# A hybrid retention, S5 and cross-attention block: who issues the rope's swap transfers, when the retention transposes are written, and the S5 matrices made in two halves

## The chip, the cores and the metric

The kernel runs on one core of one Trainium2 chip. The core has TensorE (PE, matrix products), VectorE (DVE), ScalarE (ACT), GpSimd (POOL) and SyncE (SP), which here does nothing but issue transfers. Each engine works through its own instructions in a fixed order. The metric is the device time of one execution in microseconds (us).

## The reference

One layer on x of 1024 x 1024 in float32, cut to what matters here:

```
h = rms_norm(x, norm1_g);  q, k, v, g_ret, u, g_s5 = split(h @ w_in)
q, k = rotary(q), rotary(k)              # 8 heads of 64: x1*cos - x2*sin, x1*sin + x2*cos
ret = group_norm(retention(q, k, v)) * silu(g_ret)     # chunks of 128, v heads of 128
ssm = s5(u) * silu(g_s5)                 # 64 groups of 16 channels, 64 complex states each
x = x + concat([ret, ssm]) @ w_out
x = x + cross_attention(rms_norm(x), rms_norm(mem)) @ xa_wo
return rms_norm(x, norm_f_g)
```

In S5, each group has its own discretised transition (`abar`), input matrix (`f * b`) and output matrix `c`. The kernel turns these into small matrices over blocks of time steps: powers of `abar` times B and times C, and the short convolution kernels that follow from both.

## The kernel before

All large products are made of three TensorE passes over a high and a low part of the operands (`mm3`, lines 95 to 97; `whi_`/`wlo_` are the two parts of a weight, made by ScalarE on line 74 and by VectorE or GpSimd on line 75).

A loop `for i in range(4)` goes over pairs of heads; the text calls its passes pair 0 to pair 3. Each pass projects k (`kps`) and q (`qps`), applies the rope to both, projects v (`vps`, 2 x 96 matmuls) and the gate (`gps`, 2 x 96), and then calls `retention`. The rope evicts the projection to `qs` (ACT, line 290), makes `sw`, a copy whose 32-row blocks are swapped in pairs, by four transfers (line 294), and combines them on DVE (lines 296 to 298). `retention` transposes k (`knps`), forms the chunk states (`kvps`, then `R` on DVE), the scores (`scps`, masked to `st` on DVE), the outputs (`ops`, evicted to `o` by ACT on line 536), the group norm (`mv`, `rs`, `nb`), scales `o` in 16 ACT instructions (line 554), multiplies by the gate on DVE (line 555), transposes the result (`rtps`, line 559) and stores it (`ret_d`).

`s5_prep(b)` makes the S5 matrices of block b (16 blocks of 4 groups). `s5_tables(ct)`, called at every second block, makes on POOL a table of powers (`tab`, lines 307 to 414), stores it (`tab_d`, line 417), clears a small tile (`z`, line 419) and stores that. The next table overwrites `tab`, so it starts when `tab_d` has landed. For each b POOL makes `B`, `C` and `t`; DVE makes `W` (lines 455, 457) and `VV`; PE transposes `W` (`mps`, line 460) and multiplies B by VV (`kps` with `VV`, line 470); ACT and DVE finish `Mi` and `K`. Blocks 0 to 3 are written behind pair 0's retention, 4 to 8 behind pair 1's, 9 to 13 behind pair 2's, 14 and 15 behind pair 3's. After the loop the u projection (`ups`) and the S5 scan start.

The code's order is not the order on the engines: a scheduler reorders each engine's instructions at build time, so that retention i lies under the projections of pair i+1, its `rtps` in the middle of that pair's `vps`, and S5 blocks after them. On the chip every engine keeps that order and waits in place. SP issues nearly all transfers, in one order. Transfers take one of eight completion semaphores in turn, and a transfer waits for the earlier one that holds its semaphore.

Of the kernel before, what the change touches and what calls it, by code (L numbers as in the profile page):

```python
# [12 lines left out]
F32 = mybir.dt.float32  # L13
# [7 lines left out]
P = 128  # L21
# [24 lines left out]
def block_kernel(ctx: ExitStack, tc: tile.TileContext, a: dict):  # L46
# [3 lines left out]
    def bc(ap, shape):  # L50
        return ap.to_broadcast(shape)
# [10 lines left out]
    def sm_ps(shape, name="smps"):  # L62
        return psm.tile(shape, F32, tag="sm", name=name)
# [223 lines left out]
    def rope(ps, name):  # L287
        flat = ps.rearrange("p a b -> p (a b)")
        qs = qp.tile([P, L], F32, tag="qs", name=f"qs_{name}", bufs=2)
        s.activation(qs, flat, AF.Copy)  # L290
        sw = qp.tile([P, L], F32, tag="qsw", name=f"sw_{name}", bufs=2)
        for b in range(4):
            o = 32 * (b ^ 1)
            nc.sync.dma_start(out=sw[32 * b:32 * b + 32, :], in_=qs[o:o + 32, :])
        rot = qp.tile([P, L], F32, tag="rot", name=f"rot_{name}", bufs=3)
        v.tensor_tensor(rot, qs, cosT, ALU.mult)
        v.tensor_tensor(sw, sw, sinT, ALU.mult)
        last_rope[0] = v.tensor_tensor(rot, rot, sw, ALU.add)
        return rot
# [109 lines left out]
    def s5_tables(ct):  # L409
        raw = pr.tile([P, 2, 4, GB, 16], F32, tag="bcraw", name=f"bcraw{ct}", bufs=2)  # L410
        nc.sync.dma_start(out=raw, in_=a["s5_bc"][ct])
        tab = pr.tile([P, 2, GB, SC], F32, tag="tab", name=f"tab{ct}")
        g.tensor_copy(tab[:, 0, :, 0:16], rotC[:, ct])
        g.tensor_copy(tab[:, 1, :, 0:16], rotS[:, ct])
        scr = pr.tile([P, 256], F32, tag="tg", name=f"tg{ct}")
        rotate_double(tab[:, 0], tab[:, 1], 16, SC, scr, 4)
        nc.sync.dma_start(out=a["tab_d"][ct], in_=tab)
        zero = pr.tile([P, 2, 112], F32, tag="tg", name=f"z{ct}")
        g.memset(zero, 0.0)
        nc.sync.dma_start(out=a["k_d"][ct].rearrange("(h p) t -> p h t", h=2)[:, :, 0:112], in_=zero)  # L420
        per_ct[ct] = raw

    def s5_prep(b):
        gs = slice(b * GB, b * GB + GB)
        ct, hb = b // 2, b % 2
        if hb == 0:
            s5_tables(ct)
        raw = per_ct[ct][:, hb]
        B1 = pr.tile([P, GB + 1, 16], F32, tag="B1", name=f"B1_{b}", bufs=2)
        B2 = pr.tile([P, GB, 16], F32, tag="B2", name=f"B2_{b}")  # L430
        C1 = pr.tile([P, GB, 16], F32, tag="C1", name=f"C1_{b}")
        tt = pr.tile([P, GB, 16], F32, tag="tt16", name=f"tt16_{b}")
        sh = [P, GB, 16]

        def fb(x):
            return bc(x[:, gs].unsqueeze(2), sh)
        g.memset(B1[:, GB, :], 0.0)
        g.tensor_tensor(B1[:, 0:GB], raw[:, 0], fb(FR), ALU.mult)
        g.tensor_tensor(tt, raw[:, 1], fb(FIs), ALU.mult)
        g.tensor_tensor(B1[:, 0:GB], B1[:, 0:GB], tt, ALU.add)  # L440
        g.tensor_tensor(B2, raw[:, 1], fb(FRs), ALU.mult)
        g.tensor_tensor(tt, raw[:, 0], fb(FI), ALU.mult)
        g.tensor_tensor(B2, B2, tt, ALU.subtract)
        g.tensor_scalar(C1, raw[:, 2], psgn, None, op0=ALU.mult)

        def pw(tab, n):
            return bc(tab[:, 0:n, gs].rearrange("p t g -> p g t").unsqueeze(3), [P, GB, n, 16])

        def ve(x, n):
            return bc(x.unsqueeze(2), [P, GB, n, 16])  # L450
        W1 = pr.tile([P, GB, 8, 16], F32, tag="W1", name=f"W1_{b}")
        t1 = pr.tile([P, GB, 8, 16], F32, tag="t1", name=f"t1_{b}")
        VV = pr.tile([P, GB, 9, 16], F32, tag="VV", name=f"VV_{b}", bufs=2)
        t2 = pr.tile([P, GB, 9, 16], F32, tag="t2", name=f"t2_{b}")
        v.tensor_tensor(W1, pw(PR, 8), ve(B1[:, 0:GB], 8), ALU.mult)
        g.tensor_tensor(t1, pw(PI, 8), ve(B2, 8), ALU.mult)
        v.tensor_tensor(W1, W1, t1, ALU.add)
        mp = sm_ps([P, GB, P], "mps")
        for gi in range(GB):
            nc.tensor.transpose(mp[:, gi, :], W1[:, gi].rearrange("p t q -> p (t q)"), ident)  # L460
        Mi = pr.tile([P, GB, P], F32, tag="Mi", name=f"Mi_{b}", bufs=2)
        s.activation(Mi, mp, AF.Copy)
        nc.sync.dma_start(out=a["mi_d"][b], in_=Mi)
        v.tensor_tensor(VV, pw(PR, 9), ve(C1, 9), ALU.mult)
        v.tensor_tensor(t2, pw(PI, 9), ve(raw[:, 3], 9), ALU.mult)
        v.tensor_tensor(VV, VV, t2, ALU.subtract)
        nc.sync.dma_start(out=a["vv_d"][b], in_=VV.rearrange("p g t q -> p g (t q)"))
        kp = sm_ps([P, P], "kps")
        for gi in range(GB):
            nc.tensor.matmul(kp[32 * gi:32 * gi + 32, :], B1[:, gi:gi + 2, :].rearrange("p g q -> p (g q)"),  # L470
                             VV[:, gi, 0:8, :].rearrange("p t q -> p (t q)"), start=True, stop=True)
        K = pr.tile([P, P], F32, tag="K", name=f"K_{b}", bufs=2)
        s.activation(K, kp, AF.Copy)
        v.scalar_tensor_tensor(K[:, 0:16], i16, d4[:, b:b + 1], K[:, 0:16], op0=ALU.mult, op1=ALU.add)
        nc.sync.dma_start(out=a["k_d"][ct][P * hb:P * hb + P, 112:112 + P], in_=K)


    def proj_nat(w, name, evac):
        hi, lo = w
        for n0 in range(0, NCH, 4):  # L480
# [83 lines left out]

    for i in range(4):
        w = w0 if i == 0 else get_w("w_kq", i)
        kT = rope(proj_t(w, 0, hT, name="kps"), f"k{i}")
        qT = rope(proj_t(w, 1, hT, name="qps"), f"q{i}")
        vt = qp.tile([P, NCH, 256], F32, tag="vt", name=f"vt{i}")
        silu = qp.tile([P, NCH, 256], F32, tag="silu", name=f"silu{i}")  # L570

        def ev_v(n0, ps, vt=vt, i=i):
            for n in range(4):
                for h in range(2):
                    s.activation(vt[:, n0 + n, h * P:h * P + P], ps[:, n, h * P:h * P + P], AF.Copy,
                                 scale=vs[:, n0 + n, 2 * i + h:2 * i + h + 1])

        def ev_g(n0, ps, silu=silu):
            for n in range(4):
                s.activation(silu[:, n0 + n, :], ps[:, n, :], AF.Silu, scale=r1[:, n0 + n:n0 + n + 1])  # L580

        proj_nat(get_w("w_v", i), "vps", ev_v)
        proj_nat(get_w("w_g", i), "gps", ev_g)
        retention(i, kT, qT, vt, silu)
        if i == 0:
            with tc.issue_after(last_rope[0].ins):
                s5_params()
        for b in range((0, 4, 9, 14)[i], (4, 9, 14, 16)[i]):
            s5_prep(b)
    qctx.close()  # L590
    prctx.close()

# [509 lines left out]

# [14 lines left out]
```

## Time and profile before

| | |
|---|---|
| three runs | 1187.71, 1185.93, 1185.98 us; median 1185.98 |
| profiled execution | 1183.76 us, span of its trace 1182.0 us |
| busy: PE, DVE, ACT, POOL | 1132.4 (96%), 640.4 (54%), 451.0 (38%), 284.6 (24%) us |
| mean granted TensorE clock | 0.979 of full speed |

The span is the time from the first to the last instruction of the trace; all positions below are us from its start. Busy time of PE counts matmuls at whatever clock they ran, so a stall is visible as idle time and a slow stretch as a granted clock below 1.

### The profile page before, as it was taken

Reading aid. Unit: us, or ns where it says so; the run is one execution under the profiler, and the core shown is the slowest. Engines: PE = TensorE matmul, PEld = TensorE weight load, DVE = VectorE, ACT = ScalarE, POOL = GpSimd, SP = SyncE. Lnnn points to the kernel's source line nnn. Section 1 sums busy time; section 2 is a strip of 40 time slices with the busy share of each in tenths; the row PEclk is TensorE's granted clock in tenths of the full one; section 3 lists DMA queues with packets and bytes.
Section 4 is the critical chain, followed back from the end, with each engine's and each line's share of the span. In section 5 each row is a group of like instructions: output and inputs, shape, how many; then the busy total and the mean of one; then the engine's idle time right before and its main releaser. Section 6 shows DMA issues by size and latency. Waiting matters only on the chain.

```text
span 1182.0 us, 18361 instructions
## 1 busy us (share of the span) xinstructions
PE 1132.4 (96%) x7020; PEld 991.8 (84%) x7020; DVE 640.4 (54%) x1348; ACT 451.0 (38%) x903; POOL 284.6 (24%) x422
## 2 busy tenths in 40 slices
PE   8899689999999689999999999999999999999996
PEld 6897688898888568888888888888889888889996
DVE  7794464573662425585577216534635445554564
ACT  7322432342432312354453115224334444444453
POOL 2348798372084101212221100000320000000000
PEclk9899899999999889999999999999999999999998
DMA  6412343343241177799785349534446522222251
GB/s 233 120 52 89 98 159 131 101 153 97 55 165 58 36 225 202 212 279 276 222 268 202 133 148 279 179 124 148 137 143 197 173 77 72 72 72 72 90 197 72
DMA packets 92376, 171.88 MB, mean 145 GB/s; under 512 B 10880, under 2 KB 46976, under 8 KB 92288
## 3 DMA queue, kind: packets, MB, share of 16 engines
q1 hardware_dynamic: 92000, 170.57, 45.7%
q8 instruction: 55, 0.90, 0.3%
q14 instruction: 33, 0.27, 0.1%
q10 hardware_dynamic: 288, 0.14, 0.0%
HBM read 122.04 MB, written 44.43 MB: 141 GB/s over the span
## 4 chain that ended last, share of the span: by engine, by line
PE 59%; DMA 2%; DVE 2%; ACT 1%; issue 0%; DVEq 0%; ACTq 0%
PE wops L95 3%; PE wops L96 3%; PE wops L97 3%; PE qaps L97 3%; PE qaps L96 3%; PE gsps L97 2%; PE glups L95 2%; PE glups L97 2%; PE qaps L95 2%; PE gsps L96 2%; PE gsps L95 2%; PE obps L96 2%; PE obps L95 2%; PE obps L97 2%; PE glups L96 2%; PE oaps L97 2%
## 5 line engine op out<-in xcount | busy, mean ns | idle before, releaser
L95 PE MATMUL vps<-whi_w_v,hh 128*128 128x256 f32 x256 | 73.5, 287 | 0.7 <-ACT qs_k L290 0.7
L96 PE MATMUL vps<-wlo_w_v,hh 128*128 128x256 f32 x256 | 73.5, 287 | 0.6 <-POOL wlo_w_v L75 0.6
L95 PE MATMUL wops<-whi_w_xo,o 128*128 128x256 f32 x256 | 73.6, 288 | 0.0
L97 PE MATMUL vps<-whi_w_v,hl 128*128 128x256 f32 x256 | 73.5, 287 | 0.0
L97 PE MATMUL wops<-whi_w_xo,o 128*128 128x256 f32 x256 | 72.1, 281 | 0.0
L95 PE MATMUL gps<-whi_w_g,hh 128*128 128x256 f32 x256 | 71.9, 281 | 0.0
L96 PE MATMUL wops<-wlo_w_xo,o 128*128 128x256 f32 x256 | 71.8, 281 | 0.0
L97 PE MATMUL gps<-whi_w_g,hl 128*128 128x256 f32 x256 | 71.8, 281 | 0.0
L96 PE MATMUL gps<-wlo_w_g,hh 128*128 128x256 f32 x256 | 71.5, 279 | 0.0
L844 POOL TENSOR_TENSOR sq<-sq,sqx 128x1024 f32<-128x1024 f32 x7 | 19.0, 2717 | 196.9 <-ACT sqx L843 196.9
L95 PE MATMUL ups<-hh,whi_w_u 128*128 128x512 f32 x128 | 51.9, 406 | 1.9 <-DVE ut L692 1.9
L95 PEld LDWEIGHTS vps<-whi_w_v,hh 128*128 128x128 f32 x256 | 49.8, 194 | 1.8 <-ACT qs_k L290 1.1
L96 PE MATMUL ups<-hl,whi_w_u 128*128 128x512 f32 x128 | 51.2, 400 | 0.0
L97 PE MATMUL ups<-hh,wlo_w_u 128*128 128x512 f32 x128 | 51.2, 400 | 0.0
L96 PEld LDWEIGHTS vps<-wlo_w_v,hh 128*128 128x128 f32 x256 | 49.8, 195 | 1.6 <-POOL wlo_w_v L75 0.8
L95 PE MATMUL oaps<-reth,whi_w_oa 128*128 128x512 f32 x128 | 51.0, 398 | 0.0
L97 PE MATMUL qaps<-h,wlo_w_xq 128*128 128x512 f32 x128 | 50.6, 396 | 0.0
L95 PE MATMUL gsps<-hh,whi_w_gs 128*128 128x512 f32 x128 | 50.6, 395 | 0.0
L97 PE MATMUL gsps<-hh,wlo_w_gs 128*128 128x512 f32 x128 | 50.6, 395 | 0.0
L95 PE MATMUL qaps<-h,whi_w_xq 128*128 128x512 f32 x128 | 50.5, 394 | 0.0
L96 PE MATMUL qaps<-h,whi_w_xq 128*128 128x512 f32 x128 | 50.4, 394 | 0.0
L97 PE MATMUL oaps<-reth,wlo_w_oa 128*128 128x512 f32 x128 | 50.3, 393 | 0.0
(394 smaller groups left out, 3496.2 us busy)
## 6 DMA issues: line engine op xcount, KB each, us to landing
CS<-tab_d SPq DMA_DIRECT2D x32, 256.0 KB, 5.2
yr<-y_d SPq DMA_DIRECT2D x16, 512.0 KB, 6.2
wraw_w_xq<-w_xq SPq DMA_DIRECT2D x16, 512.0 KB, 4.1
wraw_w_xo<-w_xo SPq DMA_DIRECT2D x16, 512.0 KB, 4.4
vv_d<-VV SPq DMA_DIRECT2D x16, 288.0 KB, 2.8
VV<-vv_d SPq DMA_DIRECT2D x16, 288.0 KB, 4.3
wraw_w_v<-w_v SPq DMA_DIRECT2D x8, 512.0 KB, 4.6
wraw_w_g<-w_g SPq DMA_DIRECT2D x8, 512.0 KB, 4.8
```

What stands on the lines that cost most here:

```text
L95: nc.tensor.matmul(out, wh, xh, start=first, stop=False)
L96: nc.tensor.matmul(out, wh, xl, start=False, stop=False)
L97: nc.tensor.matmul(out, wl, xh, start=False, stop=last)
L844: g.tensor_tensor(sq2, sq2, sq, ALU.add)
```

## The change

Three edits. In `rope` the four swap transfers are issued by ScalarE, not SyncE. `retention` ends with the gated `o`; its transposes and stores are a new function `ret_store`, called in the next pass behind that pair's k projection (for pair 3 behind the first u projection, which is written before it). `s5_prep` is cut in two: the new `s5_prep` makes W and VV, `s5_finish` does the PE part and the stores, and `s5_hook`, called at sixteen points of the projections of pairs 1 to 3 and once behind the loop, finishes block b-1 and prepares block b. POOL's `B` and `C` are made once for two blocks, inside `s5_tables`. A reserved scratch area shrinks from 1024 to 512 bytes.

```diff
-            nc.sync.dma_start(out=sw[32 * b:32 * b + 32, :], in_=qs[o:o + 32, :])
+            nc.scalar.dma_start(out=sw[32 * b:32 * b + 32, :], in_=qs[o:o + 32, :])
...
-        per_ct[ct] = raw
+        gs = slice(ct * 2 * GB, ct * 2 * GB + 2 * GB)
+        sh = [P, 2, GB, 16]
+        B1 = pr.tile([P, 2 * GB + 1, 16], F32, tag="B1", name=f"B1_{ct}", bufs=2)
...
+        g.tensor_tensor(b1, raw[:, :, 0], fb(FR), ALU.mult)
...
+        per_ct[ct] = raw, B1, B2, C1
...
+        v.tensor_tensor(VV, VV, t2, ALU.subtract)
+        return W1, VV, B1
+
+    def s5_finish(b, prep):
+        W1, VV, B1 = prep
...
+    def s5_hook():
+        b = sdone[0]
+        sdone[0] += 1
+        if 0 < b <= NB:
+            s5_finish(b - 1, spreps.pop(b - 1))
+        if b < NB:
+            spreps[b] = s5_prep(b)
...
             evac(n0, ps)
+            hook()
...
             v.tensor_tensor(o[:, h], o[:, h], silu[:, :, h * P:h * P + P], ALU.mult)
+        return o
+
+    def ret_store(i, o):
+        for h in range(2):
...
         kT = rope(proj_t(w, 0, hT, name="kps"), f"k{i}")
+        if i:
+            ret_store(i - 1, o_last)
+        hook = s5_hook if i >= 1 else no_hook
+        if i >= 2:
+            hook()
         qT = rope(proj_t(w, 1, hT, name="qps"), f"q{i}")
+        if i >= 2:
+            hook()
...
-        for b in range((0, 4, 9, 14)[i], (4, 9, 14, 16)[i]):
-            s5_prep(b)
+    w_u0 = get_w("w_u", 0)
+    u_first = proj_t(w_u0, 0, hT, name="ups")
+    ret_store(3, o_last)
+    s5_hook()
```

What stands on the engines shows three places. First SP before, in pair 1, from the table that is stored ahead of the q rope's swap (`sw_q_1628`) to the one behind it; `kq_50` is a load of the next pair's k and q weights:

```order
L417 DMA tab_d<-tab_2303 128x1024
L420 DMA k_d<-z_2326 128x2x112
L70 DMA wraw_w_kq_50_1865<-w_kq 128x1024
L294 DMA sw_q_1628<-qs_q_1626 32x1024 x4
L70 DMA wraw_w_kq_51_1871<-w_kq 128x1024
```

and ACT after, at the same place:

```order
L290 ACTIVATE qs_q_1410<-qps 128x1024
L294 DMA sw_q_1412<-qs_q_1410 32x1024 x4
L577 ACTIVATE o_923<-o_923,nb_1041,rs_1040 128x128 x16
L613 ACTIVATE vt_1421<-vps,vs 128x128 x8
```

The four transfers have left SP's order, where a table's store stood ahead of them, and stand on ACT directly behind the eviction that they read, ahead of the 16 scalings.

Second, PE in the changed kernel from pair 1's retention transposes on (of `rtps` and `mps` alone; 17 `vps` stand between the two `rtps` rows, and the rest of the `vps` or 96 `gps` before each `mps`):

```order
L586 MATMUL rtps<-cp,o_923 128x128 x8
L586 MATMUL rtps<-cp,o_923 128x128 x8
L475 MATMUL mps<-cp,W_0_1582 128x128 x4
L475 MATMUL mps<-cp,W_1_1715 128x128 x4
L475 MATMUL mps<-cp,W_2_1898 128x128 x4
```

The first `rtps` stands behind 122 `vps` before and behind 125 after, so `ret_store` moves nothing much on PE. Of the S5 blocks, pair 1's projections now hold three (four before), pair 2's six (five), pair 3's six (five), the end of the loop one (two), and they stand farther apart.

Third, DVE after, from block 3's `W` to the second masked score `st` of pair 1's retention, which lies under pair 2's k and q projections:

```order
L462 TENSOR_TENSOR W_3_2027<-PR,B_1_1886 128x512
L465 TENSOR_TENSOR VV_2393<-PR,C_2_2381 128x576
L464 TENSOR_TENSOR W_3_2027<-W_3_2027,t_3_2028 128x512
L467 TENSOR_TENSOR VV_2393<-VV_2393,t_4_2394 128x576
L75 TENSOR_TENSOR wlo_w_v_6_2228<-wraw_w_v_60_2229,whi_w_v_6_2227 128x512 x2
L466 TENSOR_TENSOR t_5_2482<-PI,bcraw_2351 128x576
L75 TENSOR_TENSOR wlo_w_v_6_2228<-wraw_w_v_61_2235,whi_w_v_6_2227 128x512 x2
L486 SCALAR_TENSOR_TENSOR K_2023<-cp,K_2023 128x16
L529 SCALAR_TENSOR_TENSOR R_2050<-R_2050,cp 128x128 x4
L544 TENSOR_TENSOR st_2087<-scps,cp 128x512
L529 SCALAR_TENSOR_TENSOR R_2050<-R_2050,cp 128x128
L544 TENSOR_TENSOR st_2089<-scps,cp 128x512
```

Before, blocks 3 and 4 both stood ahead of `R` there. POOL now makes `t_3` behind the sixth table, two places behind its `z`:

```order
L441 TENSOR_SCALAR C_2_2381<-bcraw_2351,cp 128x128
L419 MEMSET z_3462 128x224
L463 TENSOR_TENSOR t_3_2028<-PI,B_1_1887 128x512
```

So a wait for `t_3` now stands ahead of `R` and `st`; and POOL's order is the first five tables, `t_2`, the sixth table, `t_3`, then the seventh (with `t_4` near its end) and the eighth.

## Rows read from the trace of the kernel before

**Rows 1.** Waits of PE: engine, what waits, for whom: us, times, longest

```profile
PE rtps L559 <- DVE o L555: 22.0, 3, 10.6
PE mps L460 <- DVE W L457: 5.8, 3, 3.3
PE ups L95 <- DVE ut L692: 1.9, 1, 1.9
...
PE mps L460 <- DVE K L474: 1.4, 1, 1.4
PE ops L531 <- DVE mv L540: 1.3, 1, 1.3
```

**Rows 2.** Timeline of PE: start, us, instruction, idle before it and its releaser

```profile
148.78 1.97 PE L559 MATMUL rtps<-cp,o 128*128 128x128 f32 x8 [10.57 <-DVE o L555]
...
238.43 1.03 PE L559 MATMUL rtps<-cp,o 128*128 128x128 f32 x8
```

**Rows 3.** Timeline of DVE in pair 1

```profile
112.58 1.44 DVE L297 TENSOR_TENSOR sw_k<-sw_k,sinT 128x1024 f32<-128x1024 f32 x1 [7.79 <-DMA sw_k<-qs_k]
...
132.66 0.66 DVE L550 SCALAR_TENSOR_TENSOR nb<-mv,rs 128x16 f32<-128x16 f32 x1
144.13 1.37 DVE L297 TENSOR_TENSOR sw_q<-sw_q,sinT 128x1024 f32<-128x1024 f32 x1 [10.81 <-DMA sw_q<-qs_q]
...
147.09 3.30 DVE L555 TENSOR_TENSOR o<-o,silu 128x1024 f32<-128x1024 f32 x2
```

**Rows 4.** Timeline of SP in pair 1 (issue of transfers)

```profile
134.83 0.32 SPq L417 DMA_DIRECT2D tab_d<-tab  x1
...
136.61 2.74 SPq L294 DMA_DIRECT2D sw_q<-qs_q  x4
```

**Rows 5.** Timeline of ACT: its first transfer, and pairs 1 and 2

```profile
0.74 0.41 ACTq L188 DMA_DIRECT2D gp<-g  x1
...
126.28 1.01 ACT L290 ACTIVATE qs_q<-qps 128x1024 f32<-128x1024 f32 x1
133.41 6.31 ACT L554 ACTIVATE o<-o,nb,rs 128x128 f32<-128x128 f32 x16 [6.13 <-DVE nb L550]
...
209.12 1.09 ACT L536 ACTIVATE o<-ops 128x512 f32<-128x512 f32 x2 [4.23 <-PE ops L534]
```

**Rows 6.** Windows: us, busy PE (x) PEld (x) DVE (x) ACT (x) POOL (x), PEclk, DMA share, GB/s

```profile
149.00:152.00 3.00, 3.00 (x17) 3.00 (x17) 1.39 (x1) 1.38 (x2) 0.60 (x2) 0.56 0.60 217
...
356.00:360.00 4.00, 4.00 (x21) 4.00 (x22) 2.83 (x5) 0.49 (x2) 3.91 (x6) 0.57 0.19 70
```

**Rows 7.** Timeline of POOL: starts and ends of tables; a `t`

```profile
123.08 0.24 POOL L413 COPY tab<-rotC 128x64 f32<-128x64 f32 x1 [2.47 <-DMA tab_d<-tab]
...
134.87 0.29 POOL L419 MEMSET z<- 128x224 f32 x1
...
152.08 0.24 POOL L413 COPY tab<-rotC 128x64 f32<-128x64 f32 x1 [2.42 <-DMA tab_d<-tab]
...
171.06 0.28 POOL L419 MEMSET z<- 128x224 f32 x1
...
352.96 1.10 POOL L456 TENSOR_TENSOR t<-PI,B 128x512 f32<-128x512 f32 x1
```

**Rows 8.** Timeline of PE, pair 1's retention under pair 2's projections

```profile
188.78 1.03 PE L494 MATMUL knps<-cp,rot_k 128*128 128x128 f32 x8
...
205.49 1.05 PE L531 MATMUL ops<-vt,st 128*128 128x128 f32 x8
...
216.67 0.38 PE L531 MATMUL ops<-vt,st 128*128 128x128 f32 x2
```

**Rows 9.** Timeline of DVE, pair 1's retention and later

```profile
199.41 2.05 DVE L506 SCALAR_TENSOR_TENSOR R<-R,cp 128x128 f32<-128x128 f32 x4 [4.65 <-ACT R L504]
...
214.65 0.65 DVE L521 TENSOR_TENSOR st<-scps,cp 128x512 f32<-128x512 f32 x1
...
250.09 0.78 DVE L457 TENSOR_TENSOR W<-W,t 128x512 f32<-128x512 f32 x1
```

More of the change, by code (lines that the diff above doesn't have):

```diff
@@ L420, in s5_tables, with fb, hg @@
         nc.sync.dma_start(out=a["k_d"][ct].rearrange("(h p) t -> p h t", h=2)[:, :, 0:112], in_=zero)
-        per_ct[ct] = raw
+        gs = slice(ct * 2 * GB, ct * 2 * GB + 2 * GB)
+        sh = [P, 2, GB, 16]
+        B1 = pr.tile([P, 2 * GB + 1, 16], F32, tag="B1", name=f"B1_{ct}", bufs=2)
+        B2 = pr.tile([P, 2 * GB, 16], F32, tag="B2", name=f"B2_{ct}")
+        C1 = pr.tile([P, 2 * GB, 16], F32, tag="C1", name=f"C1_{ct}")
+        tt = pr.tile([P, 2, GB, 16], F32, tag="tt16", name=f"tt16_{ct}")
+        def fb(x):
+            return bc(x[:, gs].rearrange("p (h g) -> p h g", h=2).unsqueeze(3), sh)
+        def hg(x):
+            return x.rearrange("p (h g) q -> p h g q", h=2)
+        b1, b2 = hg(B1[:, 0:2 * GB]), hg(B2)
+        g.memset(B1[:, 2 * GB, :], 0.0)
+        g.tensor_tensor(b1, raw[:, :, 0], fb(FR), ALU.mult)
+        g.tensor_tensor(tt, raw[:, :, 1], fb(FIs), ALU.mult)
+        g.tensor_tensor(b1, b1, tt, ALU.add)
+        g.tensor_tensor(b2, raw[:, :, 1], fb(FRs), ALU.mult)
+        g.tensor_tensor(tt, raw[:, :, 0], fb(FI), ALU.mult)
+        g.tensor_tensor(b2, b2, tt, ALU.subtract)
+        g.tensor_scalar(hg(C1), raw[:, :, 2], psgn, None, op0=ALU.mult)
+        per_ct[ct] = raw, B1, B2, C1
     def s5_prep(b):
@@ L427, in s5_prep @@
             s5_tables(ct)
[L428 to L444, printed above, removed]
+        raw, B1, B2, C1 = per_ct[ct]
+        ks = slice(hb * GB, hb * GB + GB)
+        raw, B2, C1 = raw[:, hb], B2[:, ks], C1[:, ks]
         def pw(tab, n):
@@ L454, in s5_prep @@
         t2 = pr.tile([P, GB, 9, 16], F32, tag="t2", name=f"t2_{b}")
-        v.tensor_tensor(W1, pw(PR, 8), ve(B1[:, 0:GB], 8), ALU.mult)
+        v.tensor_tensor(W1, pw(PR, 8), ve(B1[:, ks], 8), ALU.mult)
         g.tensor_tensor(t1, pw(PI, 8), ve(B2, 8), ALU.mult)
         v.tensor_tensor(W1, W1, t1, ALU.add)
+        v.tensor_tensor(VV, pw(PR, 9), ve(C1, 9), ALU.mult)
+        v.tensor_tensor(t2, pw(PI, 9), ve(raw[:, 3], 9), ALU.mult)
+        v.tensor_tensor(VV, VV, t2, ALU.subtract)
+        return W1, VV, B1
+    def s5_finish(b, prep):
+        W1, VV, B1 = prep
+        ct, hb = b // 2, b % 2
         mp = sm_ps([P, GB, P], "mps")
@@ L463, in s5_prep @@
         nc.sync.dma_start(out=a["mi_d"][b], in_=Mi)
-        v.tensor_tensor(VV, pw(PR, 9), ve(C1, 9), ALU.mult)
-        v.tensor_tensor(t2, pw(PI, 9), ve(raw[:, 3], 9), ALU.mult)
-        v.tensor_tensor(VV, VV, t2, ALU.subtract)
         nc.sync.dma_start(out=a["vv_d"][b], in_=VV.rearrange("p g t q -> p g (t q)"))
@@ L469, in s5_prep @@
         for gi in range(GB):
-            nc.tensor.matmul(kp[32 * gi:32 * gi + 32, :], B1[:, gi:gi + 2, :].rearrange("p g q -> p (g q)"),
+            nc.tensor.matmul(kp[32 * gi:32 * gi + 32, :], B1[:, hb * GB + gi:hb * GB + gi + 2, :].rearrange("p g q -> p (g q)"),
                              VV[:, gi, 0:8, :].rearrange("p t q -> p (t q)"), start=True, stop=True)
@@ L475, in s5_prep, with proj_nat @@
         nc.sync.dma_start(out=a["k_d"][ct][P * hb:P * hb + P, 112:112 + P], in_=K)
-    def proj_nat(w, name, evac):
+    spreps, sdone = {}, [0]
+    def s5_hook():
[5 more added lines that the diff above has]
+            spreps[b] = s5_prep(b)
+    def proj_nat(w, name, evac, hook):
         hi, lo = w
@@ L563, in retention, with no_hook @@
                                   in_=rt.rearrange("p a b -> p (a b)"))
+    def no_hook():
+        pass
+    o_last = None
     for i in range(4):
@@ L580, in ev_g @@
                 s.activation(silu[:, n0 + n, :], ps[:, n, :], AF.Silu, scale=r1[:, n0 + n:n0 + n + 1])
-        proj_nat(get_w("w_v", i), "vps", ev_v)
-        proj_nat(get_w("w_g", i), "gps", ev_g)
-        retention(i, kT, qT, vt, silu)
+        proj_nat(get_w("w_v", i), "vps", ev_v, hook)
+        proj_nat(get_w("w_g", i), "gps", ev_g, hook)
+        o_last = retention(i, kT, qT, vt, silu)
         if i == 0:
@@ L684, in block_kernel @@
     for gi in range(4):
-        w = get_w("w_u", gi)
+        w = get_w("w_u", gi) if gi else w_u0
         for c in range(2):
             ct = 2 * gi + c
-            ps = proj_t(w, c, hT, name="ups")
+            ps = proj_t(w, c, hT, name="ups") if ct else u_first
             ut = ev.tile([P, 8, 8, 16], F32, tag="ut", name=f"ut{ct}", bufs=3)
@@ L1104 @@
     arrays = host_arrays(**inputs)
-    nc = bacc.Bacc("TRN2", target_bir_lowering=False, num_devices=1, dynamic_dma_scratch_size=1024)
+    nc = bacc.Bacc("TRN2", target_bir_lowering=False, num_devices=1, dynamic_dma_scratch_size=512)
     aps = {n: nc.dram_tensor(n, z.shape, mybir.dt.from_np(z.dtype), kind="ExternalInput").ap()
```

## The prediction

> **What bounds the kernel.** PE is busy for nearly the whole span, so a change can gain only where PE waits, or where it runs slowly after a wait. I read the waits of PE first. Three waits of the retention transposes for DVE's gated `o` make 22.0 us, three waits of S5 transposes for `W` 5.8, and single waits of `ups`, `mps` (for `K`) and `ops` 1.9, 1.4 and 1.3 [rows 1]. The timeline of PE puts the longest but one detail at pair 1: 10.57 us before the transposes at 148.78 [rows 2]. Going back from there, DVE multiplied `o` by the gate from 147.09, and had stood 10.81 us in front of `sw_q` until 144.13 [rows 3]. ACT had made the transfers' input by 127.29 (126.28 + 1.01) [rows 5]. SP issued them only at 136.61, behind a table's store that waited for POOL until 134.83 [rows 4]. So the chain is POOL's table, SP's order, the swap, DVE, PE. ACT's 16 scalings were finished at 139.72 [rows 5] and were not what was late.
>
> PE pays once more behind a stall: from 149 to 152 its granted clock is 0.56, that is mostly at the lower of its two levels, 1.2 instead of 2.4 GHz, having been idle before it. This costs 3.0 x 0.44 = 1.3 us. From 356 to 360, behind the 3.3 us wait of an `mps`, it is 0.57: 1.7 us [rows 6].
>
> **The swaps on ScalarE, pair 1.** Four transfers behind `qs_q` at 0.41 us each (ACT's own issue) are out by 129 [rows 5]. SP needed 2.74 for four [rows 4]; were ACT as slow it would be 130. They landed 4.8 us after SP's last issue in pair 1 (139.35 to 144.13) [rows 3, 4], so `sw_q` is there by 134 to 135 at the latest, near DVE's `nb`, which ends at 133.32 [rows 3]. ACT's scalings start on `nb`, not on the transfers [rows 5]. `sw_k`, for which DVE waited 7.79 us [rows 3], comes earlier too, and the 1.3 us wait of `ops` [rows 1] and all behind it with it, `nb` and the scalings too: the first head is scaled half-way through 6.31 us, at 135.3, the second at 138.4. A gating takes 1.65 (3.30 for two) [rows 3], and DVE's remaining rope addition of about as long lies between the two: gated at 137.0 and 140.2. PE reaches the first `rtps` at 138.21 (148.78 - 10.57) - 1.3 + 0.3 (three more `vps`) = 137.2 and the second, 8 transposes of 1.03 [rows 2] and 17 `vps` later, at about 140.2. So the stall goes: -10.6, -1.3 of slow clock, -1.3 of `ops` = **-13.2**. Bounds: -8 if the transfers land 5 us later than I take, and nothing beyond -13.2.
>
> Here a rule speaks against the change. The row shows that moving the issue takes the swap out of a queue where it stood 9.3 us (127.29 to 136.61) [rows 4, 5]. The Trainium skill (DMA: Bandwidth & Descriptors, "Issuing engines are not separate DMA queues") says that transfers started by several engines run on the same DMA engines, and that issuing from more of them saves only the issuer's own time, usually small beside the transfer. By that rule pair 1 would gain the 2.74 us of issue and not 10.6; what stood in the queue here was a wait for POOL and no transfer, so I go by the rows and keep the other as a rival.
>
> In pairs 0, 2 and 3 PE waits for no rope transfer [rows 1], so the swaps there gain 0. SP's freed time gains nothing either.
>
> **The retention transposes.** PE's order shows them after 125 `vps` instead of 122: nothing, since the scheduler had already put them there. In the tail the stall of 10.2 us has the same order before and after and stays.
>
> **The S5 halves.** Of the three waits of `mps` for `W`, two (together 5.8 - 3.3 = 2.5 us) are in pair 1, where blocks followed each other every few us; 96 matmuls now lie between them: **-2.5** (0 to -2.5). The third is in pair 3, at a `W` that waited for POOL's `t` at 352.96 [rows 7], behind seven small `B`/`C` instructions and two `wlo_w_u`. The wider instructions leave about 3.5 us less ahead of `t_13`: of the 3.3 and the 1.7 of slow clock I take **-4.0** (0 to -5). In the tail one block is left, so the 1.4 of `mps` for `K` and part of the 1.9 of `ups`, whose DVE input stood behind that `K`, can go: **-1.4** (0 to -3.3). The PE work itself is moved, not removed.
>
> **What it gives back.** PE reaches pair 1's `knps` at 188.78 [rows 8] less 13.2, 2.5 and one block of about 1 us that has moved on: 172.1. `ops` then wants its masked scores at 205.49 - 16.7 = 188.8, and the second `ops` at 216.67 - 16.7 = 200.0 [rows 8]. But POOL does not come earlier: nothing of its table chain hung on PE. A table takes 11.8 us (123.08 to 134.87) plus 2.7 for its store to land [rows 7]. The fifth starts at 152.08 [rows 7] and so ends near 163.9; `t_2` follows; the sixth starts at 166.6, with some 1.5 us of `B`/`C` ends at 179.9, and `t_3` at about 181.2. DVE, which had stood for `t_3`, then has W, VV, `t_5` and four `wlo` at 0.78 each, 5.5 us, `R` 2.8 and two `st` of 0.65 [rows 9]: the second `st` is ready at 190.8, 2.0 us too late (two tables stand ahead of it: 0 if they take 10.8, 4 if they take 12.8).
>
> A second wait is not in the diff. The program's semaphores make the fourth `sw_k` transfer of pair 2, now on ACT, wait until the seventh table's store has landed, and the evictions of `ops` stand behind it. The seventh table starts at 182.6, holds two more POOL instructions of 1.5 us together, ends near 195.9 and has landed near 198.6. The evictions, wanted at 194, then start at 199. From the eviction to the second `st` of the next half took 6.2 us (209.12 to 215.30) [rows 5, 9]: 205.2, against 200.0 + 2.0: 3.2 us more (0 to 6). The eighth table's store, on which `sw_q` of pair 2 depends in the same way, should have landed at 213, before its `qs_q` is ready (`ops` at 202 and more than 10 us of projection): 0. With 1 us of slow clock behind the two waits (0 to 3) the give-back is **+6.2** (0 to 13).
>
> **The sum.** -13.2 - 2.5 - 4.0 - 1.4 + 6.2 = -14.9. The profiled execution took 1183.76 us, 2.2 less than the median of the runs, 1185.98; I subtract from the median: 1171.1, and 1168.9 for a profiled run.
>
> **Rivals.**
> - *No give-back.* If the tables run some 1.7 us faster each (three stand ahead of the 5.2 us), both waits in pair 2 vanish: 1171.1 - 6.2 = 1164.9, and with the S5 waits gone in full 1162. For it: POOL no longer has as many small instructions among its tables. Against it: the next table waits for the store of the last, and POOL shares time with a DVE that is now busier earlier.
> - *Only the issue is saved.* The swap arrives no sooner than its transfer allows, and pair 1 gains 2.7 + 1.3 instead of 13.2. PE then comes 9 us later to the tables, so there is no give-back: -4.0 - 2.5 - 4.0 - 1.4 = -11.9, 1174; with the S5 gains at half, 1178. Against it: the 9.3 us in SP's order, which no transfer filled.
> - *Slower: the tables become the bound.* In the stretch where `B`, `C` and `t` ran among it, a table took 19.0 us (152.08 to 171.06) [rows 7]. If the fifth to seventh stay as slow, the fifth ends at 171, the sixth at 193, `t_3` at 194.2 and the second `st` at 203.8: 15 us of waiting. The seventh lands at 217.2, ACT is held until then, and the second `ops` starts at 223.8 instead of 215: 9 more. With 3 us of slow clock 27 stand against gains of 21.1, so 1192. Each us per table costs 3 (three tables ahead of the second wait), so it turns where tables take about 4 us more than I take, 16 us for the fifth. Against it: only some ten such instructions remain among these tables.
>
> **Chances and range.** Forecast 0.48 (1166 to 1177 by its own terms), no give-back 0.24, only the issue 0.14, slower 0.08, and 0.06 for a mixture that ends near the old time. Runs of before differ by 1.8 us; a difference under 0.2%, 2.4 us, is no difference that a measurement here can tell. Faster by more: 0.48 + 0.24 + 0.14 + 0.02 = 0.88; within it 0.04; slower 0.08. The range takes in the first three cases, from 1160 (2 us under the best case, 1162, for what these terms leave out) to 1182 (issue alone, and the S5 gains at 0).
>
> **What would show it.** Right: at pair 1's first `rtps` no wait over 1 us, the window behind it at full clock; under pair 2's projections waits of PE for `st` of 1 to 6 us, with ACT idle before an `o` eviction until a `tab_d` store; no `mps` wait in pair 1, and under 1 us in pair 3; the 10 us stall in the tail as before. Wrong: DVE still idle at `sw_q` beyond 136 in pair 1, waits of PE over 10 us in pair 2, or a table over 16 us.

## The result, and the profile after

| | before | after |
|---|---|---|
| median of the runs | 1185.95 us (4 runs, 1184.03 to 1187.71) | 1175.29 us (4 runs, 1174.82 to 1177.57) |
| profiled execution, span | 1183.76, 1182.0 us | 1175.01, 1173.2 us |
| mean granted TensorE clock | 0.979 | 0.981 |

The ratio is 0.9912, 95% interval 0.9899 to 0.9924. The change is faster by 10.7 us: inside the range and 4.2 us short of the forecast. The profiled execution, 1175.01 us, is 6.1 us above the 1168.9 forecast for one. The waits of PE after (columns as in [rows 1]):

```profile
PE rtps L586 <- DVE o L578: 14.4, 4, 10.2
...
PE ops L554 <- DVE st L544: 4.4, 1, 4.4
PE ups L95 <- DVE ut L732: 1.8, 1, 1.8
PE mps L475 <- DVE W L464: 1.7, 2, 1.5
```

Of the 22.0 us of `rtps` in [rows 1], 14.4 are left, and a wait of `ops` for `st` is new. The timeline of PE shows where:

```profile
138.02 1.03 PE L586 MATMUL rtps<-cp,o 128*128 128x128 f32 x8
...
172.28 0.98 PE L517 MATMUL knps<-cp,rot_k 128*128 128x128 f32 x7
...
189.05 1.05 PE L554 MATMUL ops<-vt,st 128*128 128x128 f32 x8
...
204.57 0.77 PE L554 MATMUL ops<-vt,st 128*128 128x128 f32 x2 [4.41 <-DVE st L544]
...
233.70 1.09 PE L586 MATMUL rtps<-cp,o 128*128 128x128 f32 x8 [1.54 <-DVE o L578]
...
321.99 1.09 PE L586 MATMUL rtps<-cp,o 128*128 128x128 f32 x8 [1.48 <-DVE o L578]
...
349.74 0.63 PE L475 MATMUL mps<-cp,W 128*128 128x128 f32 x4 [1.50 <-DVE W L464]
...
407.46 1.94 PE L586 MATMUL rtps<-cp,o 128*128 128x128 f32 x8 [10.20 <-DVE o L578]
```

Against [rows 2, 8]: the first `rtps` came 10.76 us earlier, `knps` 16.50, the second `ops` 12.10 and pair 2's `rtps` only 4.73. So pair 1 gained nearly all that was forecast, and pair 2 gave back 11.8 of it. The timelines of DVE and ACT in pair 1 show the first half of the story:

```profile
130.98 0.38 DVE L573 SCALAR_TENSOR_TENSOR nb<-mv,rs 128x16 f32<-128x16 f32 x1
131.29 1.21 DVE L297 TENSOR_TENSOR sw_q<-sw_q,sinT 128x1024 f32<-128x1024 f32 x1
134.62 1.42 DVE L578 TENSOR_TENSOR o<-o,silu 128x1024 f32<-128x1024 f32 x1 [2.13 <-ACT o L577]
```

```profile
126.41 2.45 ACTq L294 DMA_DIRECT2D sw_q<-qs_q  x4
...
188.47 9.72 ACTq L294 DMA_DIRECT2D sw_k<-qs_k  x4
198.24 1.09 ACT L559 ACTIVATE o<-ops 128x512 f32<-128x512 f32 x2 [9.80 <-DMA tab_d<-tab]
...
221.15 2.51 ACTq L294 DMA_DIRECT2D sw_q<-qs_q  x4
```

The q swap was issued at 126.41 instead of 136.61 [rows 4], and DVE, which had stood 10.81 us in front of it [rows 3], now takes it right behind `nb`. In pair 2 the same four instructions took ACT 9.72 us instead of 2.45, and the eviction of `ops` behind them ended its wait with the store of a table, as forecast. DVE has the swapped `k` ahead of the second half's `st` in its order, so it then waited for the held transfer itself:

```profile
201.91 1.65 DVE L297 TENSOR_TENSOR sw_k<-sw_k,sinT 128x1024 f32<-128x1024 f32 x1 [1.95 <-DMA sw_k<-qs_k]
...
203.76 0.67 DVE L544 TENSOR_TENSOR st<-scps,cp 128x512 f32<-128x512 f32 x1
```

SP issued the table's store at 194.10, when POOL had finished the table (the second row, two loads of weights, bears on the run f3 below):

```profile
194.10 0.33 SPq L417 DMA_DIRECT2D tab_d<-tab  x1
...
220.08 1.62 SPq L70 DMA_DIRECT2D wraw_w_kq<-w_kq  x2
```

The windows show the price on PE (columns as in [rows 6]):

```profile
138.00:152.00 14.00, 14.00 (x127) 13.63 (x126) 4.33 (x6) 3.54 (x10) 8.63 (x22) 1.00 0.53 170
...
204.00:217.00 13.00, 12.43 (x41) 9.43 (x42) 5.95 (x28) 1.09 (x2) 4.31 (x6) 0.50 0.13 49
```

Behind pair 1's `rtps` the clock is full (1.00; 0.56 in [rows 6]). From 204 to 217, behind the 4.41 us in which PE had been idle, the granted clock is 0.50, the lower of the two levels, 1.2 GHz, for the whole 13 us. PE looks fully busy there, and does half the work.

### The profile page after: what moved, and what is told of

It reads as the page before. It is cut to its first block, busy times and chain, and to the rows that moved or that the text cites. A ratio compares the mean times of both kernels' runs of the same rounds, so it can differ in the third digit from the quotient of the medians.

```text
span 1173.2 us, 18247 instructions
## 1 busy us (share of the span) xinstructions
PE 1132.9 (97%) x7020; PEld 990.3 (84%) x7020; DVE 649.0 (55%) x1348; ACT 449.7 (38%) x903; POOL 267.7 (23%) x358
## 4 chain that ended last, share of the span: by engine, by line
PE 71%; DMA 9%; POOL 8%; DVE 7%; ACT 2%; issue 2%; SPq 0%; ACTq 0%; DVEq 0%; POOLq 0%
PE wops L96 3%; PE wops L97 3%; PE wops L95 3%; PE qaps L95 3%; PE gsps L97 3%; PE qaps L97 3%; PE qaps L96 3%; PE gsps L96 3%; PE gsps L95 2%; PE obps L96 2%; PE obps L97 2%; PE obps L95 2%; PE ups L95 2%; PE ups L96 2%; PE ups L97 2%; PE glups L97 2%
## 5 line engine op out<-in xcount | busy, mean ns | idle before, releaser
L96 PE MATMUL gsps<-hl,whi_w_gs 128*128 128x512 f32 x128 | 50.3, 393 | 0.0
L97 PE MATMUL glups<-yh,wlo_w_glu 128*128 128x512 f32 x128 | 50.2, 392 | 0.0
```

The source lines that it names most:

```text
L96: nc.tensor.matmul(out, wh, xl, start=False, stop=False)
L97: nc.tensor.matmul(out, wl, xh, start=False, stop=last)
```

## The experiments

Positions of the same PE instruction in the traces that the argument rests on (us from the start; the last `rtps` follows the loop; "`ups`" is the first behind the first `Sps` of the S5 scan). "Swaps alone" is e1_swap_only. "Halves alone" is e2_swap_sp; it has every edit but the swaps, so the wider `B` and `C` of POOL and the new places of the blocks are in it too, and no run separates these:

| | before | after | swaps alone | halves alone | e3 | h1 | h2 |
|---|---|---|---|---|---|---|---|
| `knps` of pair 1 | 188.78 | 172.28 | 187.16 | 184.26 | 174.21 | 173.03 | 169.68 |
| its second `ops` | 216.67 | 204.57 | 215.05 | 212.19 | 202.43 | 200.96 | 206.82 |
| `rtps` in pair 2 | 238.43 | 233.70 | 238.58 | 233.43 | 225.96 | 224.37 | 228.09 |
| `rtps` in pair 3 | 324.63 | 321.99 | 325.99 | 320.10 | 314.49 | 313.20 | 316.05 |
| last `rtps` | 411.93 | 407.46 | 413.12 | 405.33 | 400.02 | 398.82 | 401.70 |
| `ups` | 447.96 | 440.13 | 449.10 | 438.43 | 432.97 | 431.81 | 435.67 |
| span | 1182.0 | 1173.2 | 1182.8 | 1174.2 | 1171.2 | 1167.2 | 1172.4 |

The theory I began with: the swaps bring pair 1's 13 us, the halves 8, and POOL's tables, through ACT's order, take part of it back in pair 2. Rivals: only the issue is saved, or the halves alone do it all.

**e1_swap_only**: the kernel before with only the swaps moved.

```diff
-            nc.sync.dma_start(out=sw[32 * b:32 * b + 32, :], in_=qs[o:o + 32, :])
+            nc.scalar.dma_start(out=sw[32 * b:32 * b + 32, :], in_=qs[o:o + 32, :])
```

> The kernel before with the first edit alone: the swap transfers issued by ScalarE, nothing else. Theory: pair 1's 10.6 us wait and the 1.3 us of slow clock behind it came from the swap standing behind a table's store on SyncE, so they go here too (first retention transposes of pair 1 near 138 instead of 148.8), and the 1.2 us wait of ops with them. Still there: the two S5 waits in pair 1 (2.5 us) and the 3.3 us one in pair 3. New: some wait of ScalarE in pair 2 behind a table's store, since its transfers share the semaphores, 0 to 4 us of it seen by TensorE. About 1174 to 1177. Rival (the gain needs the new places of the S5 blocks and of the transposes; the issuer saves only its own issue time): pair 1 still waits 7 us or more, 1181 or above.

1187.07 us, ratio 1.0009 (0.9996 to 1.0023): no gain at all. The stall of `rtps` did go: they start at 137.73, 11.05 us earlier. The timelines of PE, ACT and SP show what took its place:

```profile
154.23 0.65 PE L470 MATMUL kps<-VV,B 128*32 128x128 f32 x8 [7.09 <-ACT rt L561]
...
165.30 0.52 PE L460 MATMUL mps<-cp,W 128*128 128x128 f32 x3 [3.35 <-DVE W L457]
```

```profile
153.40 0.69 ACT L561 ACTIVATE rt<-rtps,cp 128x512 f32<-128x512 f32 x1 [11.86 <-DMA ret_d<-rt]
```

```profile
149.48 0.33 SPq L417 DMA_DIRECT2D tab_d<-tab  x1
149.90 0.39 SPq L420 DMA_DIRECT2D k_d<-z  x1
150.37 1.88 SPq L562 DMA_DIRECT2D ret_d<-rt  x3
```

PE reached the next things that hang on the same tables. ACT's `rt` needed a buffer whose store stood in SP's order behind the fourth table, and block 2's `W` needed a `t` that POOL makes in the midst of the fifth. At `knps` 1.62 us were left of 13. My theory's number fell here; the rival's number was met, but by another mechanism than the one it named.

**e2_swap_sp**: the changed kernel with the swaps back on SyncE.

```diff
-            nc.scalar.dma_start(out=sw[32 * b:32 * b + 32, :], in_=qs[o:o + 32, :])
+            nc.sync.dma_start(out=sw[32 * b:32 * b + 32, :], in_=qs[o:o + 32, :])
```

> The changed kernel with the first edit undone: swaps on SyncE, transposes and S5 halves as changed. Theory: the q swap of pair 1 stands behind a table's store again, so TensorE waits 10 us for the first retention transposes of pair 1, and the S5 halves give what they gave (2.5 in pair 1, some 2 in pair 3, some 3 in the tail); no wait for the second ops in pair 2, because TensorE comes there 12 us later. About 1178 to 1182. Rival (the S5 halves and the moved transposes made the gain): 1175 or less, with no wait over 3 us in pair 1.

1177.06 us, ratio 0.9918 (0.9890 to 0.9946), just below the range of the theory and above that of the rival. The other edits alone give 8.9 us, and their interval takes in the changed kernel's ratio, 0.9912: by the times, the halves may have made the whole gain. In the table this kernel reaches pair 1's `knps` 12 us later than the changed one, and pair 2's `rtps` at the same time. Its trace also has a slow stretch of its own (timeline and windows, PE):

```profile
117.15 0.51 PE L554 MATMUL ops<-vt,st 128*128 128x128 f32 x2 [2.29 <-DVE mv L563]
...
147.97 1.41 PE L586 MATMUL rtps<-cp,o 128*128 128x128 f32 x6 [4.88 <-DVE o L578]
```

```profile
117.00:128.00 11.00, 10.85 (x39) 8.19 (x40) 3.73 (x25) 1.09 (x2) 8.04 (x21) 0.53 0.17 60
```

That `rtps` waits only 4.88 us here, against 10.57 in [rows 2], is no gain of the halves: PE came later, by the slow stretch.

The retention transposes need no run: written back at the end of `retention` in the changed kernel, they leave all five engines' orders the same, row by row.

**e3_tab_pool**: the changed kernel with the tables stored by GpSimd, which makes them.

```diff
-        nc.sync.dma_start(out=a["tab_d"][ct], in_=tab)
+        nc.gpsimd.dma_start(out=a["tab_d"][ct], in_=tab)
```

> The changed kernel, with the eight table stores issued by GpSimd instead of SyncE; they no longer share completion semaphores with ScalarE's transfers. Theory: the 4.4 us wait of the second ops in pair 2 and the 5.8 us of slow clock behind it come from ScalarE held at its fourth sw_k transfer until the seventh table has landed, with the evictions of ops behind it. That hold goes here, so ScalarE's idle time before the o eviction at 198 is under 1 us, the second ops does not wait, and the time is 7 to 11 us less: 1164 to 1168. Rival (the masked scores are late because POOL's tables or the landing of sw_k are late by themselves, not through ScalarE's order): the wait of the second ops stays over 3 us and the time within 3 us of 1175. Open cost: what issuing eight transfers takes on GpSimd; if 1 us or more each, the tables end later and t_3 can be late for pair 2's first masked scores.

1171.98 us, ratio 0.9883 (0.9853 to 0.9913): 4 us above the theory's range. The mechanism came as expected. With the table's store out of SP's order and its semaphores, ACT is not held and the clock stays up (timeline of ACT; window as above):

```profile
190.40 3.90 ACTq L294 DMA_DIRECT2D sw_k<-qs_k  x4
194.88 1.09 ACT L559 ACTIVATE o<-ops 128x512 f32<-128x512 f32 x2 [4.51 <-PE ops L557]
```

```profile
204.00:217.00 13.00, 13.00 (x100) 11.81 (x100) 7.89 (x37) 5.06 (x10) 6.71 (x13) 1.00 0.37 100
```

The window holds 100 matmuls against 41 (not quite the same ones: e3 is 2 us further on in the order there). This shows the hold as the cause of the new wait, of which e3's later arrival could explain 1.9 us at most, and the slow clock as the larger part of its price: at pair 2's `rtps` e3 is 7.7 us ahead of the changed kernel, although `knps` is 1.9 later. The runs show 3.4 us of it (ratios 0.9883 and 0.9912, whose intervals overlap). In the profiled execution some 3.5 us of the lead over before are lost between 598 and 631, where ACT waits 6.3 us for the retention's rows to come back from memory and PE stands 3.2 us in two waits; the cause was not tried.

**e5_b_tab_pool**: the kernel before with the stores of tables and zero tiles (lines 417 and 420) on GpSimd and the swaps left on SyncE, so that the swap no longer stands behind a table.

```diff
-        nc.sync.dma_start(out=a["tab_d"][ct], in_=tab)
+        nc.gpsimd.dma_start(out=a["tab_d"][ct], in_=tab)
...
-        nc.sync.dma_start(out=a["k_d"][ct].rearrange("(h p) t -> p h t", h=2)[:, :, 0:112], in_=zero)
+        nc.gpsimd.dma_start(out=a["k_d"][ct].rearrange("(h p) t -> p h t", h=2)[:, :, 0:112], in_=zero)
```

> The kernel before, with the stores of the tables and of the cleared tiles issued by GpSimd; the swaps stay on SyncE, where no table's store stands ahead of them any more. Theory: what was late in pair 1 was the order on SyncE and not the issuer, so the wait of the retention transposes goes from 10.6 us to under 2 us as with the swaps on ScalarE, and the k swap of pair 1 comes early too: 1172 to 1176. Rival (ScalarE's own queue, or its shorter issue, is what made the swap fast): pair 1 still waits over 5 us, 1180 or above.

1185.03 us, ratio 0.9988 (0.9974 to 1.0003), no gain again. The theory was right on the wait, so what had been late was the order on SP and not the issuer; its time was 9 us off. The `rtps` start at 139.01 without a wait, and 23 us later (PE, POOL):

```profile
161.93 1.09 PE L460 MATMUL mps<-cp,W 128*128 128x128 f32 x4 [8.98 <-DVE W L457]
```

```profile
159.89 1.10 POOL L456 TENSOR_TENSOR t<-PI,B 128x512 f32<-128x512 f32 x1
```

The stall moved to block 2's `t`, in the midst of the fifth table on POOL; at `knps` 2.53 us were left.

**g1_pool_order**: e5 with the swaps on ScalarE too, and with the fifth table put behind block 3's `t` on GpSimd.

```diff
-        if hb == 0:
+        if ct == 4 and hb == 0:
+            with tc.issue_after(tins[3].ins):
+                s5_tables(ct)
+        elif hb == 0:
             s5_tables(ct)
```

> The kernel before, its S5 blocks where they were, with the swaps on ScalarE, the stores of tables and cleared tiles issued by GpSimd, and the fifth table held behind block 3's t in GpSimd's order. Theory: with the swaps early but the old places of the S5 blocks, the 13 us gained at pair 1's retention transposes were lost a few us later, at S5 blocks whose t stood behind the fifth table on GpSimd, and at an rt eviction that waited for a store behind a table on SyncE; with both taken away the S5 blocks of pair 1 wait 4 us at most, so 8 us or more remain at pair 1's knps (which is then at 181 or earlier): 1174 to 1179. Rival (the old places of the blocks are too close together for DVE itself): knps of pair 1 is within 4 us of the old 188.8 and the time above 1182.

1180.57 us, ratio 0.9954 (0.9937 to 0.9972), between the ranges of theory and rival. Block 2's `t` ends at 155.78 instead of 160.99, the wait of `mps` is 5.52 instead of 8.98, `knps` comes 8.57 us earlier than before instead of 2.53, and now a part of the gain reaches the end. Of the 6 us more at `knps` some 1.6 may be the swaps' (the first `rtps` at 137.44 instead of 139.01). So in the kernel before, pair 1's stall was worth what POOL's order let through.

**f3_load_behind**: e3 with the first loads of the next weights issued by ScalarE behind the q swap. Pairs 2 and 3 of the changed kernel wait 1.54 and 1.48 us for a `sw_q` that landed 6.4 us after its last issue (timeline of DVE), behind two loads of 512 KB each that SP issued from 220.08 on (above):

```profile
230.02 1.23 DVE L297 TENSOR_TENSOR sw_q<-sw_q,sinT 128x1024 f32<-128x1024 f32 x1 [5.91 <-DMA sw_q<-qs_q]
```

```diff
+            if nm == "w_kq" or (nm, ix) == ("w_u", 0):
+                with tc.issue_after(swap_q[0].ins):
+                    wstate["next"] = load_w(a[nm][ix], f"{nm}{ix}_{n}", lo_eng, nc.scalar)
```

> The kernel of the run with the table stores on GpSimd, and the next pair's k and q weights (two loads of 512 KB, also the first u weights) issued by ScalarE behind the q swap instead of by SyncE ahead of it. Theory: the new waits of 1.5 to 2.0 us for the retention transposes of pairs 2 and 3 come from the q swap, whose transfers land some 6 us after issue because 1 MB of weights was issued just ahead and all run on the same DMA engines; behind the swap the weights leave it free, it lands within 3 us, and both waits go: 3 to 4 us less at the end of pair 3 than in that run, 1168 to 1171 in all if nothing later takes it back. Rival (the scalings on ScalarE, late by the four issues, are what those transposes wait for): both waits stay at 1.5 us or more.

1177.92 us, ratio 0.9920 (0.9894 to 0.9946). The two waits went, as expected: the swap of pair 2 landed 1.9 us after its last issue, not 6.4. But the second `ops` waited 7.2 us and the time is 7 us above the theory's range; by the medians the run lost what e3 had won, though the intervals overlap. POOL, SP and ACT:

```profile
188.74 0.30 POOL L426 MEMSET z<- 128x224 f32 x1
```

```profile
189.07 0.38 SPq L427 DMA_DIRECT2D k_d<-z  x1
189.53 0.63 SPq L486 DMA_DIRECT2D vv_d<-VV  x1
```

```profile
191.71 5.78 ACTq L301 DMA_DIRECT2D sw_k<-qs_k  x4
197.54 1.09 ACT L566 ACTIVATE o<-ops 128x512 f32<-128x512 f32 x2 [9.91 <-DMA sw_k<-qs_k]
```

PE had come 2.7 us earlier than in e3, SP still stood for the zero tile that POOL clears behind each table, and ACT's transfers waited for those that stand behind it in SP's order and hold their semaphores. h2 below, without the zero tile, has no such hold.

**f4_tail_gate**: the changed kernel with GpSimd's low part of the third u weight held until the last `nb` is made.

```diff
+            if fence[0] is not None and (nm, ix) == ("w_u", 2):
+                with tc.issue_after(fence[0].ins):
+                    wstate["next"] = load_w(a[nm][ix], f"{nm}{ix}_{n}", g)
...
+        if i == 3:
+            gate = small.tile([P, 1], F32, tag="gate", name="gate")
+            fence[0] = g.tensor_copy(gate, nb[:, 0:1])
```

> The changed kernel, with the third u weight's low part on GpSimd held back until the last group norm's nb is made (a one-column copy of nb on GpSimd ahead of it). Theory: in the tail four small DVE instructions of the group norm take 1.2 us instead of 0.2 because GpSimd's 1.2 us instructions on wide tiles run beside them, which makes the 10.2 us wait of the last transposes 4 us longer than it need be; held back, the wait is about 6 us and the time 4 to 5 us less than the changed kernel's: 1170 to 1172. Rival (the small instructions are slow for another reason, as the wait for an operand): they still take over 1 us and the wait stays at 10.

1175.35 us, ratio 0.9916 (0.9893 to 0.9939): no change against the changed kernel, although the last wait of `rtps` fell from 10.20 to 6.90, as the theory had it; the next wait, of `ups`, rose from 1.80 to 3.01, and where the rest went was not followed. It shows one thing of the hardware, below.

**f5_all**: e3, f3 and f4 together.

> The changed kernel with all three: table stores on GpSimd, the k and q weights behind the q swap, and the gate in the tail. If the three causes are right and independent, the gains add to those of the single runs: 1164 to 1168, below both kernels; if the last part of the S5 scan is bound by something that does not come earlier, as it seemed when TensorE came there 15 us early, some 3 to 4 us of it are lost there: 1167 to 1170.

1172.96 us, ratio 0.9882 (0.9861 to 0.9903); the second `ops` waits 7.83 us as in f3. No better than e3, and above both ranges.

**h1_zero_once**: e3 with one zero tile for all stores, so that no zero store in SP's order waits for a table.

```diff
-        zero = pr.tile([P, 2, 112], F32, tag="tg", name=f"z{ct}")
-        g.memset(zero, 0.0)
+        if ct == 0:
+            zc[0] = pr.tile([P, 112], F32, tag="zc", name="zc")
+            g.memset(zc[0], 0.0)
...
-        nc.sync.dma_start(out=a["k_d"][ct].rearrange("(h p) t -> p h t", h=2)[:, :, 0:112], in_=zero)
+        nc.sync.dma_start(out=a["k_d"][ct].rearrange("(h p) t -> p h t", h=2)[:, :, 0:112],
+                          in_=bc(zc[0].unsqueeze(1), [P, 2, 112]))
```

> The changed kernel with the tables' stores issued by GpSimd (as in e3_tab_pool) and with the zero tile that starts each k_d made once, so that none of the eight zero stores stands behind a table on GpSimd. Theory: GpSimd's table chain bounds pairs 1 and 2, and what reached TensorE from it there were transfers in SyncE's order behind the tables; with none left, second ops of pair 2 come without a wait or under 2 us of one, each table ends up to 1 us sooner because it has no memset ahead of it, and the run comes out at 1168 to 1173 us (e3_tab_pool was 1171.98). The rtps waits of pairs 2 and 3 (2.0 and 1.7 us in e3_tab_pool) stay, since the q swap still lands behind the weights' load. Rival: in e3_tab_pool no wait was left at second ops, so nothing is to be had here; the zero stores cost nothing and the time is that of e3_tab_pool within 2 us.

1171.01 us, ratio 0.9884 (0.9865 to 0.9902). The time is in the theory's range, but the ratio is e3's, so the rival stands: the zero stores cost e3 nothing that its runs can tell. The trace's 4 us less of span is one execution.

**h2_zero_load**: h1 with f3's loads.

> h1_zero_once with the raw loads of w_kq and of the first w_u issued by ScalarE behind the q swap (as in f3_load_behind, where the rtps waits of pairs 2 and 3 went, but second ops of pair 2 waited 7.2 us because ScalarE's k swap was held by stores that stood in SyncE's order behind the sixth zero tile). Theory: with the zero tile made once nothing in that order hangs on a table, so both gains come together: no rtps wait in pairs 2 and 3, second ops of pair 2 with less than 2 us of wait, 1165 to 1170 us. Rival: the k swap's transfers are held by something else (stores of VV and K matrices of the S5 block), second ops of pair 2 wait 5 us or more again, and the time stays at 1174 to 1178 us.

1172.66 us, ratio 0.9893 (0.9868 to 0.9918). That lies between the two ranges. ACT's four transfers take 2.45 us again, with no hold, and pairs 2 and 3 have no `rtps` wait, as the theory had it; but the first `ops` now wait for `st`, and the clock falls. PE, DVE and POOL, and the window:

```profile
190.48 1.18 PE L563 MATMUL ops<-vt,st 128*128 128x128 f32 x4 [3.89 <-DVE st L553]
```

```profile
178.11 0.96 DVE L474 TENSOR_TENSOR VV<-PR,C 128x576 f32<-128x576 f32 x1 [7.16 <-POOL C L450]
...
189.65 0.69 DVE L553 TENSOR_TENSOR st<-scps,cp 128x512 f32<-128x512 f32 x1
```

```profile
178.42 1.61 POOL L472 TENSOR_TENSOR t<-PI,B 128x512 f32<-128x512 f32 x1
```

```profile
190.00:203.00 13.00, 11.98 (x57) 9.80 (x58) 9.13 (x25) 1.09 (x2) 7.71 (x18) 0.61 0.35 95
```

PE is 2.6 us earlier at `knps` than in the changed kernel. DVE, standing 7.16 us for POOL, starts its string of work for `st` too late. Neither theory of this run had that wait. It is the first of the two that the prediction had put into pair 2, and it ends on POOL's table chain again.

## Why the prediction was right, and where it missed

**Right.** The bound (PE, which loses where it waits), the chain behind pair 1's stall, and its size: `rtps` at 138.02 against 137.2 forecast, `knps` at 172.28 against 172.1, no `mps` wait in pair 1, and full clock behind it. The q swap was issued 10.2 us earlier, since what the queue had held was a wait for a table and no transfer. By the rule of the Trainium skill (DMA: Bandwidth & Descriptors, "Issuing engines are not separate DMA queues"), that issuing from more engines saves only the issuer's own time, an estimated 2.7 us would have come; the trace does not agree. The second place was right too: ACT held in front of its fourth swap transfer until a table's store had landed, the eviction at 198.24 (forecast 199), the second `ops` at 204.57 (forecast 205.2). That this second number fits is in part luck: I had the eviction alone between the hold and `st`, but DVE then stood 1.95 us more for the held swap, and `st` came behind that.

**Mis-sized: the give-back, +6.2.** It measured 11.8 us to pair 2's `rtps` (16.50 less 4.73), and pair 3's waited 1.48 more. Term by term:
- The lateness of `st`, 2.0, was 0: the fifth and sixth tables took 10.7 and 11.0 us (151.89 to 162.61, 165.69 to 176.66), not 11.8 and 13.3, and block 3's `t` ended at 178.47, not 181.2. My terms had 0 for tables of 10.8. The wait came in h2, where PE was 2.6 us earlier and that `t` 1.6 later. POOL:

```profile
176.91 1.56 POOL L463 TENSOR_TENSOR t<-PI,B 128x512 f32<-128x512 f32 x1
```

- The hold on ACT, 3.2, was 4.4 of waiting. With the first term these make 5.2 forecast, 4.4 measured.
- Slow clock, 1.0 (bound 3), was about 5.8: 12.10 of lead at the second `ops` less 4.73 at `rtps`, less 1.54 waited there. This is the step that failed; with the 1.5 of the next term it makes the 5.6 by which the give-back was too small. I had priced it by [rows 6], where the clock was back within 3 us after a 10.57 us stall; here it stayed at the lower level for 13 us after 4.41 us.
- `sw_q` of pair 2, 0: I asked only whether its semaphore was free, not which loads were issued ahead of it. It came late enough for 1.5 us of wait in pairs 2 and 3 each, and with the loads behind it (f3) the waits went.

**The S5 halves, -7.9 in all.** Pair 3 took 39.8 us from its `rtps` to its `knps` instead of 41.6, with one block of some 0.9 us more in it, so it gained about 2.8 against 4.0. The slow clock behind the wait went (0.57 in [rows 6]):

```profile
350.00:360.00 10.00, 10.00 (x91) 9.63 (x90) 4.35 (x6) 0.77 (x2) 3.94 (x3) 1.00 0.22 80
```

But a wait of 1.50 stayed (forecast: under 1). In the trace DVE takes `W` there behind `VV`, whose `C` POOL had made, behind a `wlo_w_u`, until 346.1; that was read, not tried. The tail gained 3.4 (411.93 to 447.96 took 36.0 us, now 32.7) against 1.4, of which some 1 us is a block moved into the pairs. What it gained beyond the forecast hides a part of the miss in pair 2. Alone the halves made 8.9 us (e2).

**The split.** Net, I had 7.0 us for the swaps (13.2 less 6.2) and 7.9 for the rest. The runs say about 2 and 9 by the medians, 0.7 and 9.7 by the ratios (e2's 0.9918 against 0.9912, with intervals that overlap): that the swaps gained anything beside the halves is not shown. That the swaps were worth this little beside the halves, and nothing without them (e1), was not in the prediction as such; its slower rival, "the tables become the bound", named the mechanism. Its price did not come, since the fifth to seventh tables took 10.7 to 13.6 us in the changed kernel and not 19, but POOL's table chain is what PE met next in e1, e5, f3 and h2.

## What to carry to other kernels

A stall that you remove is worth only what the next waiter on the same producer lets through: before summing, list everything downstream that hangs on that producer (here POOL's tables: SP's order, S5 blocks, ACT through shared semaphores), and shift them all; no run here did that in full. A transfer issued by a busy compute engine hands that engine the transfer's waits for semaphores (four issues took ACT 9.72 us instead of 2.45 here), so look for what it holds up in each pass of the loop, not only in the one that gains. The lowest ratios here came with the producer's stores out of the common queue (e3, f5, h1: 0.988), though their intervals overlap the changed kernel's, and in the kernel before that edit gained nothing (e5).

## What the runs showed of the hardware

- The slow clock after a stall is not read from the stall's length. 10.57 us idle, followed by projection matmuls, cost 1.3 us [rows 2, 6]; 4.41 us idle ahead of the retention's small matmuls cost some 5.8 us, and 2.29 us of the same kind (e2) left the clock at 0.53 for 11 us. In f3, f4, f5 and h2, with 3.9 to 7.8 us idle ahead of the same matmuls, it was 0.50 to 0.61 for 10 to 13 us. What keeps it low there was not tried.
- Small VectorE instructions stretch beside a wide GpSimd one. In the changed kernel's tail (DVE, then POOL), and in f4, where GpSimd was kept away:

```profile
397.73 0.17 DVE L120 SCALAR_TENSOR_TENSOR rs<-t_gn,rs 128x16 f32<-128x16 f32 x1
397.94 1.17 DVE L118 TENSOR_TENSOR t_gn<-rs 128x16 f32<-128x16 f32 x1
...
401.59 1.19 DVE L573 SCALAR_TENSOR_TENSOR nb<-mv,rs 128x16 f32<-128x16 f32 x1
```

```profile
397.81 4.93 POOL L75 TENSOR_TENSOR wlo_w_u<-wraw_w_u,whi_w_u 128x512 fp32r<-128x512 f32 x4 [29.51 <-ACT whi_w_u L74]
```

```profile
396.81 0.17 DVE L578 SCALAR_TENSOR_TENSOR nb<-mv,rs 128x16 f32<-128x16 f32 x1
```

Four of GpSimd's instructions take 4.93 us, 1.23 each, and each of four tiny DVE ones beside them takes as long, 1.17 to 1.19 us instead of 0.17. The Trainium skill (SBUF — State Buffer, "SBUF: two separate sides") says that a VectorE instruction with two inputs in SBUF and a GpSimd one that reads SBUF exclude each other for a whole instruction. The rows agree.
